# One PSUM bank per sum, out of eight in turn, for the six sums of an FFN input-projection group

## The chip, the cores and the metric

The kernel runs on one core of one Trainium2 chip. The metric is the device time of one execution in microseconds (us), the median of several runs. The names of the engines follow the profile: PE is the matmul engine (PEld its weight load), DVE the vector engine, ACT the scalar engine, POOL and SP the two that mostly issue DMAs here.

## What is computed

One inference step of a two-layer streaming encoder on 1024 prompt frames and 64 frames of a running stream, float32 in and out. Each layer is a mixer (layer 0: Mamba-2 SSD beside a gated short convolution; layer 1: a gated linear recurrence) and then a gated convolutional FFN. The change lies in the FFN, which both layers have:

```python
D_MODEL = 1024; D_FF = 2816; FFN_CONV = 3; DEPTH = 2
def conv_ffn(h, st, w_in, conv_w, conv_b, w_out):
    gu = h @ w_in                                  # (1088, 1024) @ (1024, 5632)
    g, u = gu[..., :D_FF], gu[..., D_FF:]
    g, new_st = causal_dwconv(g, conv_w, conv_b, st)
    return (jax.nn.gelu(g) * u) @ w_out, new_st
x = x + conv_ffn(rmsnorm(x, norm_ffn[l]), ...)
```

## The kernel before, in words

Activations lie transposed, 128 channels on the partitions and T = 1092 tokens along the free dimension (1024 prompt, 4 of padding, 64 of the running stream). Every float32 operand is split into a high and a low half, and each product is three matmuls (high by high, low by high, high by low).

Inside an FFN, `ffn` (L907) goes through 44 half-layers, called **groups** here, 22 in each layer: for each of 11 pairs of 128-channel tiles first a *gate* group (u = 0) and then an *up* group (u = 1). One group multiplies a 2 x 2 block of weight tiles with the two halves of the token axis by a Strassen-Winograd scheme of seven products. The function `seven` (L432) holds it. The products W, Z1, Z2, X1, X2, X3 and Y are each 12 matmuls of 428 columns; V1 and V0 are the 236 tokens left over, each 24 matmuls of 236 columns. That is 84 matmuls of 428 columns and 48 of 236 in a group.

They go to six sums: `pw` (W), `v1` (V1), `v0` (V0), `px` (X1, then X2 on top, then X3 on top), `py` (Y) and `pz` (Z1, then Z2 on top). Before the change the six lie in two PSUM tiles of three banks each, L436 to L438:

```python
        ta, tb = psum(), psum()
        pw, v1, v0 = ta[:, 0, 0:SB], ta[:, 1, 0:RB], ta[:, 2, 0:RB]
        px, py, pz = tb[:, 0, 0:SB], tb[:, 1, 0:SB], tb[:, 2, 0:SB]
```

`psum()` takes from the pool `pm`, which has two such tiles (six of the eight banks); the other two banks are the pool `pa` for `aux()`.

The order of the work is written out by hand. Inside the loop over groups `in_order(True)` (L82) chains the instructions of PE, DVE and ACT to the order of the code, each engine for itself. In a middle group (mode "mid", L484) PE's order is W, V1, Z1, X1, V0, Y, X2, Z2, X3. Between them stand, for DVE and ACT:

- `held(ps)` (L448), an ACT copy of a sum to SBUF (tile `cp`): of `pw` after V1, of `pz` after X1, of `px` after V0 (named p1) and of `px` again after X2 (named u2).
- `plain(m, v)`, a DVE multiplication of `v1` or `v0` into a work tile `wk`.
- `put(m, b, ps, t)`, a DVE addition of a sum and a held copy into `wk`: of `py` and p1 before X2, of `pz` and u2 after Z2, and twice of `px` after X3.
- `nxt.step()` (L397), the next quarter of the next group's weights in tiles `ring`: an ACT copy, a DVE subtraction, and in the first two quarters two more DVE additions. The ring has eight tiles, all eight in use by one group, so that a quarter can be made only when the products that used its tile are through.
- `pending`: what the previous group left, for a gate group its scaling and convolution (`convs`, L931) and its GELU (`gelus`, L942), for an up group the multiplication with the gate and the store to `h_d` (`gated`, L958).

The first group of a layer (mode "first", L504) has another order and holds `rs()`, the RMS norm's sums of squares (matmuls `pa<-ss,ones`) with a chain of ACT and DVE steps behind them (`rstd`, L256). The last group (L528) has another order too. Behind the groups stands the output projection, `chunks` (L570), whose matmuls read `wh` and `wl` and write tiles of `psum()`.

Of the kernel before, what the change touches and what calls it, by code (L numbers as in the profile page):

```python
# [1 line left out]

# [6 lines left out]
F = mybir.dt.float32  # L9
# [4 lines left out]
P = 128  # L14
# [7 lines left out]
NB = 3  # L22
BL = T // NB

SB = 428
RB = T - 2 * SB
# [30 lines left out]
def program(nc, tc, a, ctx):  # L57
# [24 lines left out]
    def in_order(on):  # L82
        order["on"] = on
        for e in (V, S, TE):
            e.last = None
# [2 lines left out]
    sl = ctx.enter_context(tc.tile_pool(name="sl", bufs=1))  # L88
    wp = ctx.enter_context(tc.tile_pool(name="wp", bufs=1))
    sm = ctx.enter_context(tc.tile_pool(name="sm", bufs=1))  # L90
    pm = ctx.enter_context(tc.tile_pool(name="pm", bufs=2, space=bass.MemoryType.PSUM))
    pa = ctx.enter_context(tc.tile_pool(name="pa", bufs=2, space=bass.MemoryType.PSUM))
    dram = ctx.enter_context(tc.tile_pool(name="dram", bufs=1, space=bass.MemoryType.DRAM))

    n_of = {}
# [30 lines left out]

    def psum():
        n_of["pm"] = n_of.get("pm", 0) + 1
        return pm.tile([P, NB, 512], F, tag="pm", name=f"pm{n_of['pm']}")

    def aux():
        n_of["pa"] = n_of.get("pa", 0) + 1
        return pa.tile([P, 4, P], F, tag="pa", name=f"pa{n_of['pa']}")

    def scratch(name, shape):
        return dram.tile(shape, F, name=name, tag=name)
# [47 lines left out]
    def step():  # L184
        if between:
            try:
                next(between[0])
            except StopIteration:
                between.pop(0)
# [115 lines left out]
    class Next:  # L305
# [25 lines left out]
        def rs(self):  # L331
            return rms(self.ss[0], D, self.ss[1])
# [99 lines left out]
    def seven(ws, X, group, pending, nxt, mode="mid", rs=None):  # L432


        put, plain = group
        ta, tb = psum(), psum()  # L436
        pw, v1, v0 = ta[:, 0, 0:SB], ta[:, 1, 0:RB], ta[:, 2, 0:RB]
        px, py, pz = tb[:, 0, 0:SB], tb[:, 1, 0:SB], tb[:, 2, 0:SB]  # L438

        def mul(ps, w, half, name, start=True, ks=range(HK)):  # L440
            for k in ks:
                at = slice((half * HK + k) * P, (half * HK + k + 1) * P)
                wh, wl = ws.w[w][0][:, at], ws.w[w][1][:, at]
                xh, xl = X.part(name, k)
                for i, (wx, x) in enumerate(((wh, xh), (wl, xh), (wh, xl))):
                    TE.matmul(ps, wx, x, start=start and k == 0 and i == 0, stop=k == HK - 1 and i == 2, skip_group_check=True)

        def held(ps):  # L448
            n = n_of["cp"] = n_of.get("cp", 0) + 1
            t = wp.tile([P, 512], F, tag="wh", bufs=4, name=f"cp{n}")[:, 0:SB]  # L450
            S.activation(t, ps, AF.Copy)
            return t

        def V1():
            mul(v1, "a2", 0, "k0")
            mul(v1, "a2", 1, "k1", False)

        def V0():
            mul(v0, "a1", 0, "k0")
            mul(v0, "a1", 1, "k1", False)  # L460

        def W():
            mul(pw, "a2", 1, "t4")

        def Z1():
            mul(pz, "s31", 1, "t1")

        def Z2():
            mul(pz, "s24", 1, "b22", False)

        def X1():
            mul(px, "a1", 0, "b11")

        def X2():
            mul(px, "s24", 0, "t2", False)

        def X3():
            mul(px, "s31", 0, "t3", False)

        def Y():  # L480
            mul(py, "a1", 1, "b21")

        step = nxt.step if nxt is not None else lambda: None
        if mode == "mid":  # L484
            W()
            pending[0]()
            V1()
            w = held(pw)
            Z1()
            pending[1]()  # L490
            plain(1, v1)
            X1()
            p5 = held(pz)
            V0()
            p1 = held(px)
            step()
            plain(0, v0)
            Y()
            step()
            put(0, 0, py, p1)  # L500
            X2()
            u2 = held(px)
            Z2()
        elif mode == "first":  # L504
            ws.step()
            Y()
            mul(v1, "a2", 1, "k1")
            mul(v0, "a1", 1, "k1")
            ws.step()
            for k in range(HK):  # L510
                mul(px, "a1", 0, "b11", True, [k])
                mul(pz, "s31", 1, "t1", True, [k])
                mul(pw, "a2", 1, "t4", True, [k])
                mul(v1, "a2", 0, "k0", False, [k])
                mul(v0, "a1", 0, "k0", False, [k])
            p1 = held(px)
            p5 = held(pz)
            w = held(pw)
            plain(1, v1)
            plain(0, v0)  # L520
            X2()
            put(0, 0, py, p1)
            u2 = held(px)
            rs()
            step()
            step()
            Z2()
        else:  # L528
            Z1()
            pending[0]()  # L530
            X1()
            p5 = held(pz)
            W()
            p1 = held(px)
            pending[1]()
            X2()
            w = held(pw)
            V1()
            u2 = held(px)
            V0()  # L540
            plain(1, v1)
            Y()
            plain(0, v0)
            put(0, 0, py, p1)
            Z2()
        put(0, 1, pz, u2)
        step()
        X3()
        put(1, 0, px, w)
        put(1, 1, px, p5)  # L550
        step()
# [333 lines left out]
    def residual(src):  # L885
        out = []
        for m in Pairs.order:
            t = ring()
            nc.gpsimd.dma_start(t, src(m))
            out.append((m, t))  # L890
        return [t for _, t in sorted(out, key=lambda x: x[0])]
# [15 lines left out]
    def ffn(layer, X, done, after):  # L907

        kind = f"ffn{layer}"
# [7 lines left out]
        def gate(p, first):  # L917
            cbs = [conv_buffer(), conv_buffer()]
            gs = [None, None]

            def put(m, b, ps, t):
                V.tensor_add(cbs[m][:, PAD + b * SB:PAD + (b + 1) * SB], ps, t)

            def plain(m, ps):
                cb = cbs[m][:, PAD + 2 * SB:PAD + T]
                if first:
                    S.activation(cb, ps, AF.Copy)
                else:
                    V.tensor_mul(cb, ps, state["rs"][:, B[2]])

            def convs():  # L931
                RS = state["rs"]
                at = slice(0, T if first else 2 * SB)
                for cb in cbs:
                    V.tensor_mul(cb[:, PAD:][:, at], cb[:, PAD:][:, at], RS[:, at])
                for m, cb in enumerate(cbs):
                    gs[m] = wk()
                    conv_first(cb, kind, 2 * p + m, gs[m])
                for m, cb in enumerate(cbs):
                    conv_rest(cb, kind, 2 * p + m, gs[m])  # L940

            def gelus():  # L942
                for g in gs:
                    S.activation(g, g, AF.Gelu_apprx_tanh)
                    V.tensor_mul(g, g, state["rs"])

            return (put, plain), (convs, gelus), gs
# [22 lines left out]
        def ready(g):  # L970
            p, u = g
            return Ready(*[("f_in", layer, 2 * (2 * p + m) + u) for m in range(2)])

        ws = X.first
        gs, pending = None, (nothing, nothing)
        in_order(True)
        for n, (p, u) in enumerate(groups):
            nw = ready(groups[n + 1]) if n + 1 < len(groups) else None
            if u == 0:
                group, then, gs = gate(p, n == 0)  # L980
            else:
                group, then = up(p, gs)
            seven(ws, X, group, pending, nw, "first" if n == 0 else "last" if nw is None else "mid", rs)
            ws, pending = nw, then
        pending[0]()
        in_order(False)

        XR = residual(lambda m: X.spill[m])
        done.XR = XR
# [16 lines left out]
    x_d = scratch("x_d", [KT, P, T])  # L1006
    last, nxt = nxt, Next(None, "mix1", x_d)
    ffn(0, last, nxt, lambda: prefetch(("lru_in", 8)))


# [157 lines left out]
    for k in keep:  # L1168
        nc.gpsimd.dma_start(a["o_keep_" + k], keep[k].rearrange("p a b c -> p (a b c)"))
    nc.gpsimd.dma_start(a["o_lru"], keep_lru.rearrange("p a b -> p (a b)"))  # L1170

# [102 lines left out]


def build(nc, arrays):
    from contextlib import ExitStack

    ap = {k: nc.dram_tensor(k, v.shape, F, kind="ExternalInput").ap() for k, v in arrays.items()}
    for k, s in OUTS.items():
        ap[k] = nc.dram_tensor(k, s, F, kind="ExternalOutput").ap()
    with tile.TileContext(nc) as tc, ExitStack() as ctx:
        program(nc, tc, ap, ctx)
# [8 lines left out]
```

## Time and profile before

| | us |
|---|---|
| median of 3 runs (3172.82 to 3180.51) | 3174.36 |
| the profiled execution | 3177.55 |
| its span, from the first to the last instruction | 3175.7 |
| PE busy, of the span | 2811.9 (89%) |
| DVE busy | 1894.3 (60%) |
| ACT busy | 971.3 (31%) |

The profiled execution is 3.2 us (0.1%) above the median. The profile gives for each engine the time in which it ran instructions; a busy PE can still run at the lower of its two clocks, and the row PEclk shows the granted clock in tenths of the full one in 40 slices of the span. The two stretches of the FFN input projections lie at 815 to 1538 us and 2163 to 2892 us of the span.

### The profile page before, as it was taken

The page shows a single profiled execution, that of the slowest core. Times are in us where ns is not written, and L with a number is a line of the kernel's source. Part 1 is how long each engine was busy: PE and PEld are TensorE (multiplying, and loading weights), DVE is VectorE, ACT ScalarE, POOL GpSimd, SP SyncE. Part 2 cuts the span into 40 slices and gives each one's busy share as a digit, 9 for nine tenths or more (in the row PEclk, how much of TensorE's full clock was granted, in tenths as well). Part 3 has the DMA queues.
Part 4 walks back from the last instruction along what each step waited for, and adds up shares of the span by engine and source line. Part 5 has one row for each costly group of instructions (what it writes and reads, how often), then busy time and mean ns, then how long its engine had stood idle before and what let it go on. Part 6 is the DMA issues. An engine that isn't in the chain of part 4 may idle for free.

```text
span 3175.7 us, 38882 instructions
## 1 busy us (share of the span) xinstructions
PE 2811.9 (89%) x16132; PEld 2687.4 (85%) x16132; DVE 1894.3 (60%) x2199; ACT 971.3 (31%) x1296; POOL 248.5 (8%) x641
## 2 busy tenths in 40 slices
PE   8999999999877777787999999997777777879998
PEld 8999999999767776676999899997676776769997
DVE  8556566686744455454666676866444454446666
ACT  6333232222422222222211444624222222222212
POOL 1101001110100000000100100201000000001002
PEclk9999999999989898898999999998898898989999
DMA  3222222441311111111532411343111111115222
GB/s 118 85 89 80 76 78 80 143 160 64 109 48 62 48 54 41 41 68 42 192 99 68 139 55 55 103 148 103 48 68 42 49 47 41 69 41 188 95 70 70
DMA packets 81089, 260.16 MB, mean 82 GB/s; under 512 B 9584, under 2 KB 12192, under 8 KB 80912
## 3 DMA queue, kind: packets, MB, share of 16 engines
q0 software_dynamic: 35264, 133.86, 12.6%
q1 hardware_dynamic: 45360, 123.39, 11.9%
q8 instruction: 127, 2.08, 0.3%
q10 hardware_dynamic: 288, 0.42, 0.0%
q14 instruction: 50, 0.41, 0.0%
HBM read 190.36 MB, written 57.21 MB: 78 GB/s over the span
## 4 chain that ended last, share of the span: by engine, by line
PE 72%; DVE 15%; ACT 5%; issue 5%; DMA 2%; POOL 1%; DVEq 0%; SPq 0%; ACTq 0%; POOLq 0%
PE pm L70 70%; DVE wk L70 8%; DVE ring L70 3%; PE pa L70 2%; DVE raw L70 2%; ACT ring L70 2%; DVE x L70 1%; ACT wk L70 1%; ACT x L70 1%; ACT cp L70 1%; DMA wk<-h_d 1%; ACT L70 0%; DVE ss L70 0%; DMA ss<-wk 0%; DMA ring<-at_d 0%
## 5 line engine op out<-in xcount | busy, mean ns | idle before, releaser
L70 PE MATMUL pm<-x,ring 128*128 128x428 f32 (+1 forms) x5808 | 1116.4, 356 | 321.5 <-DVE wk L70 285.2
L70 PEld LDWEIGHTS pm<-x,ring 128*128 128x128 f32 x5808 | 1022.9, 210 | 413.7 <-DVE wk L70 242.9
L70 PE MATMUL pm<-x,wh 128*128 128x364 f32 x6144 | 1228.3, 331 | 7.3 <-DVE ring L70 5.4
L70 PEld LDWEIGHTS pm<-x,wh 128*128 128x128 f32 x6144 | 1043.9, 188 | 17.9 <-DVE ring L70 7.1
L70 PE MATMUL pm<-x,wl 128*128 128x364 f32 x3072 | 684.6, 329 | 0.6 <-DVE wl L70 0.6
L70 PEld LDWEIGHTS pm<-x,wl 128*128 128x128 f32 x3072 | 536.1, 188 | 1.3 <-DVE wl L70 0.9
L70 DVE TENSOR_TENSOR ring<-ring,pm 128x1092 f32<-128x1092 f32 (+2 forms) x273 | 332.3, 1222 | 197.0 <-PE pm L70 192.7
L70 DVE TENSOR_TENSOR wk<-pm,cp 128x428 f32<-128x428 f32 x176 | 101.8, 599 | 404.9 <-PE pm L70 404.9
L70 DVE TENSOR_TENSOR ring<-raw,ring 128x1024 fp32r<-128x1024 f32 x176 | 215.1, 1222 | 198.6 <-ACT ring L70 198.3
L70 ACT ACTIVATE ring<-raw 128x1024 fp32r<-128x1024 f32 x176 | 186.0, 1058 | 425.4 <-PE pm L70 407.5
L70 ACT ACTIVATE cp<-pm 128x428 f32<-128x428 f32 x176 | 87.1, 521 | 501.2 <-PE pm L70 497.2
L70 ACT ACTIVATE wh<-rawo 128x512 fp32r<-128x512 f32 x136 | 84.6, 626 | 352.2 <-PE pm L70 315.0
L70 ACT ACTIVATE wh<-raw 128x512 fp32r<-128x512 f32 x128 | 79.1, 626 | 336.2 <-PE pm L70 335.9
L70 ACT ACTIVATE x<-wk 128x1092 fp32r<-128x1092 f32 (+1 forms) x82 | 87.9, 1072 | 238.7 <-PE pm L70 202.8
L70 DVE SCALAR_TENSOR_TENSOR wk<-wk,par,wk 128x1092 f32<-128x1092 f32 x104 | 138.9, 1353 | 13.8 <-ACT wk L70 12.3
L70 DVE TENSOR_TENSOR wk<-wk,ss 128x1092 f32<-128x1092 f32 (+1 forms) x105 | 123.3, 1196 | 0.2
L70 DVE TENSOR_TENSOR x<-wk,x 128x1092 fp32r<-128x1092 f32 (+1 forms) x82 | 101.9, 1243 | 31.2 <-ACT x L70 31.2
L70 DVE TENSOR_TENSOR wk<-pm,ss 128x236 f32<-128x236 f32 (+1 forms) x75 | 61.1, 815 | 84.7 <-PE pm L70 40.8
L70 DVE TENSOR_TENSOR wl<-raw,wh 128x512 fp32r<-128x512 f32 x128 | 86.5, 682 | 40.4 <-ACT wh L70 40.4
L70 DVE TENSOR_TENSOR wl<-rawo,wh 128x512 fp32r<-128x512 f32 x136 | 91.0, 686 | 28.6 <-ACT wh L70 28.6
L70 ACT ACTIVATE wk<-wk 128x1092 f32<-128x1092 f32 x59 | 65.9, 1117 | 82.3 <-DVE wk L70 78.9
L70 DVE TENSOR_TENSOR wk<-pm,wk 128x236 f32<-128x236 f32 (+1 forms) x60 | 38.3, 641 | 86.5 <-PE pm L70 84.6
(185 smaller groups left out, 1672.3 us busy)
## 6 DMA issues: line engine op xcount, KB each, us to landing
raw<-f_in SPq DMA_DIRECT2D x88, 512.0 KB, 3.5
h_d<-wk POOLq DMA_DIRECT2D x44, 546.0 KB, 4.3
wk<-h_d POOLq DMA_DIRECT2D x42, 546.0 KB, 5.0
raw<-ab_in SPq DMA_DIRECT2D x44, 512.0 KB, 3.6
rawo<-f_out SPq DMA_DIRECT2D x88, 256.0 KB, 3.1
ss<-wk POOLq DMA_DIRECT2D x18, 546.0 KB, 5.1
ring<-at_d POOLq DMA_DIRECT2D x16, 546.0 KB, 7.0
rawo<-ab_out SPq DMA_DIRECT2D x32, 256.0 KB, 3.1
```

The source lines that it names most:

```text
L70: out = call(*args, **kwargs)
```

## The change

The six sums of a group become six tiles of one bank each, taken in turn from a pool `pb` of eight. The pools of PSUM are now opened and closed on the way: `psum_of("seven")` closes `pm` and `pa` and opens `pb` ahead of the groups of a layer, `psum_of("plain")` goes back behind them. `aux()` takes a bank of `pb` meanwhile, so that `rs()` in the first group uses three of the eight.

```diff
-    pm = ctx.enter_context(tc.tile_pool(name="pm", bufs=2, space=bass.MemoryType.PSUM))
-    pa = ctx.enter_context(tc.tile_pool(name="pa", bufs=2, space=bass.MemoryType.PSUM))
+    banks = {"stack": None, "n": 0}
+
+    def psum_of(kind):
+
+        if banks["stack"] is not None:
+            banks["stack"].close()
+        banks["stack"], banks["kind"] = ExitStack(), kind
+        banks["n"] += 1
+        for name in ("pm", "pa") if kind == "plain" else ("pb",):
+            banks[name] = banks["stack"].enter_context(tc.tile_pool(name=f"{name}_{banks['n']}", bufs=2, space=bass.MemoryType.PSUM, reuse_waits="tile"))
+
+    psum_of("plain")
...
+    def bank():
+        n_of["pb"] = n_of.get("pb", 0) + 1
+        return banks["pb"].tile([P, 512], F, tag="pb", bufs=8, name=f"pb{n_of['pb']}")
 
     def aux():
+        if banks["kind"] != "plain":
+            return bank().rearrange("p (a b) -> p a b", a=4)
...
         put, plain = group
-        ta, tb = psum(), psum()
-        pw, v1, v0 = ta[:, 0, 0:SB], ta[:, 1, 0:RB], ta[:, 2, 0:RB]
-        px, py, pz = tb[:, 0, 0:SB], tb[:, 1, 0:SB], tb[:, 2, 0:SB]
+        pw, v1, pz, px, v0, py = [bank()[:, 0:n] for n in (SB, RB, SB, SB, RB, SB)]
...
         in_order(True)
+        psum_of("seven")
         for n, (p, u) in enumerate(groups):
...
         in_order(False)
+        psum_of("plain")
```

No instruction is added or removed, and inside the groups the order on each engine is the same. What differs is the waits, and the place of nine matmuls at the end of a layer. The rows below are PE's order of instructions as built: operation, output, operands, size, and the engines whose semaphores it waits for (DVE_49, Activation_49). A sum's tile is `pm_` before and `pb_` now, `x_` is an activation tile, `ring_` a weight tile.

PE, second group of layer 0 (an up group), from the end of X1 to the start of V0, before:

```order
L70 MATMUL pm_7369<-x_7125,ring_7322 128x428
L70 MATMUL pm_7369<-x_7126,ring_7321 128x428
L70 MATMUL pm_7368<-x_6772,ring_7321 128x236 [waits DVE_49,Activation_49]
L70 MATMUL pm_7368<-x_6772,ring_7322 128x236
L70 MATMUL pm_7368<-x_6773,ring_7321 128x236
```

and now:

```order
L72 MATMUL pb_7380<-x_7125,ring_7331 128x428
L72 MATMUL pb_7380<-x_7126,ring_7330 128x428
L72 MATMUL pb_7381<-x_6772,ring_7330 128x236
L72 MATMUL pb_7381<-x_6772,ring_7331 128x236
L72 MATMUL pb_7381<-x_6773,ring_7330 128x236
```

V0's first matmul waited for DVE and ACT, readers of other banks of its tile; it has no wait now.

PE, the same group, from the end of Z2 to the start of X3, before:

```order
L70 MATMUL pm_7369<-x_7121,ring_7341 128x428
L70 MATMUL pm_7369<-x_7122,ring_7340 128x428
L70 MATMUL pm_7369<-x_6772,ring_7342 128x428 [waits DVE_49]
L70 MATMUL pm_7369<-x_6772,ring_7343 128x428
L70 MATMUL pm_7369<-x_6773,ring_7342 128x428
```

and now:

```order
L72 MATMUL pb_7379<-x_7121,ring_7350 128x428
L72 MATMUL pb_7379<-x_7122,ring_7349 128x428
L72 MATMUL pb_7380<-x_6772,ring_7351 128x428 [waits Activation_49]
L72 MATMUL pb_7380<-x_6772,ring_7352 128x428
L72 MATMUL pb_7380<-x_6773,ring_7351 128x428
```

X3 waited for a DVE reader (the `put` of `pz`); it waits for ACT alone now (the copy u2 of `px`). At X2 the same change is made: the wait for DVE (the `put` of `py`) gives way to one for ACT (the copy p1). At Z2 and Y a wait for ACT is gone.

PE, end of layer 0, from the last matmuls of Z2 on, before:

```order
L70 MATMUL pm_11105<-x_7121,ring_11081 128x428
L70 MATMUL pm_11105<-x_7122,ring_11080 128x428
L70 MATMUL pm_11323<-x_11296,wh_11315 128x364 [waits Activation_49]
L70 MATMUL pm_11323<-x_11296,wh_11315 128x364 x2
L70 MATMUL pm_11323<-x_11296,wl_11316 128x364 [waits DVE_49]
L70 MATMUL pm_11323<-x_11296,wl_11316 128x364 x2
L70 MATMUL pm_11323<-x_11297,wh_11315 128x364 [waits DVE_49]
L70 MATMUL pm_11323<-x_11297,wh_11315 128x364 x2
L70 MATMUL pm_11105<-x_6772,ring_11082 128x428 [waits DVE_49]
```

and now, from the last matmuls of X3 on:

```order
L72 MATMUL pb_11196<-x_7123,ring_11172 128x428
L72 MATMUL pb_11196<-x_7124,ring_11171 128x428
L72 MATMUL pm_11423<-x_11396,wh_11415 128x364 [waits DVE_49,Activation_49]
L72 MATMUL pm_11423<-x_11396,wh_11415 128x364 x2
L72 MATMUL pm_11423<-x_11396,wl_11416 128x364 x3
```

Nine matmuls of the output projection stood ahead of the last X3; they stand behind it now, and the first of them waits for readers of the banks. On POOL the two last stores of `h_d` come a few DMAs earlier than before among the loads of the output projection; SP's order is the same.

## Rows read from the trace of the kernel before

**Rows 1.** The page: the granted clock in 40 slices, in tenths.

```profile
PEclk9999999999989898898999999998898898989999
```

**Rows 2.** Windows of both layers: first two groups, next 18, the end.

```profile
core 0: us, PE busy (x) PEld busy (x) DVE busy (x) ACT busy (x) POOL busy (x), PEclk, DMA share, GB/s
815.14:893.14 78.00, 57.48 (x265) 51.17 (x264) 42.09 (x51) 26.27 (x35) 3.46 (x11) 0.82 0.19 49
2163.49:2241.28 77.79, 55.64 (x266) 49.89 (x265) 41.99 (x51) 27.36 (x36) 3.49 (x11) 0.85 0.17 48
893.14:1476.41 583.27, 451.35 (x2376) 414.03 (x2376) 294.83 (x342) 150.63 (x181) 21.17 (x91) 0.91 0.15 51
2241.28:2831.88 590.60, 458.73 (x2376) 420.69 (x2376) 294.87 (x342) 150.60 (x181) 19.55 (x91) 0.89 0.15 51
1476.41:1537.75 61.34, 51.96 (x286) 47.35 (x287) 31.26 (x36) 17.20 (x22) 6.77 (x18) 0.94 0.34 121
2831.88:2891.91 60.03, 51.77 (x286) 47.37 (x287) 31.28 (x36) 17.22 (x22) 6.76 (x18) 0.94 0.33 117
```

**Rows 3.** PE, layer 0, same stretches: count | busy, mean ns | idle, releasers.

```profile
L70 PE MATMUL pm<-x,ring 128*128 128x428 f32 (+1 forms) x252 | 54.0, 383 | 19.7 <-DVE wk L70 15.1 <-ACT x L70 3.2 <-DVE x L70 0.7
...
L70 PE MATMUL pm<-x,ring 128*128 128x428 f32 (+1 forms) x2376 | 451.4, 353 | 131.9 <-DVE wk L70 120.8 <-ACT cp L70 11.1
...
L70 PE MATMUL pm<-x,ring 128*128 128x428 f32 (+1 forms) x276 | 50.1, 340 | 9.0 <-DVE wk L70 6.5 <-ACT ring L70 1.0 <-DVE ring L70 0.9
```

**Rows 4.** PE's timeline, two groups: start, length, instructions [idle before, releaser].

```profile
1022.48 17.33 PE L70 MATMUL pm<-x,ring 128*128 128x428 f32 x108 [0.77 <-DVE wk L70]
1043.98 4.65 PE L70 MATMUL pm<-x,ring 128*128 128x428 f32 x12 [4.17 <-DVE wk L70]
1049.24 2.61 PE L70 MATMUL pm<-x,ring 128*128 128x428 f32 x12 [0.62 <-ACT cp L70]
1052.62 12.31 PE L70 MATMUL pm<-x,ring 128*128 128x428 f32 x72 [0.77 <-DVE wk L70]
1068.44 6.89 PE L70 MATMUL pm<-x,ring 128*128 128x236 f32 x36 [3.51 <-DVE wk L70]
1079.51 4.15 PE L70 MATMUL pm<-x,ring 128*128 128x428 f32 x12 [4.17 <-DVE wk L70]
1084.27 2.59 PE L70 MATMUL pm<-x,ring 128*128 128x428 f32 x12 [0.62 <-ACT cp L70]
```

**Rows 5.** Windows: the output projection of layer 0, and an X2.

```profile
1534.60:1786.00 251.40, 251.37 (x1503) 250.91 (x1504) 161.96 (x153) 49.63 (x66) 13.75 (x26) 1.00 0.31 107
1043.98:1048.63 4.65, 4.65 (x12) 3.82 (x12) 0.00 (x0) 0.00 (x0) 0.00 (x0) 0.50 0.00 0
```

**Rows 6.** One pair of groups: its window, two groups each of DVE and ACT.

```profile
1087.63:1152.71 65.08, 50.47 (x264) 46.38 (x265) 32.76 (x38) 16.72 (x21) 2.13 (x10) 0.90 0.15 50
...
L70 DVE TENSOR_TENSOR ring<-raw,ring 128x1024 fp32r<-128x1024 f32 x8 | 9.8, 1222 | 9.8 <-ACT ring L70 9.8
...
L70 DVE TENSOR_TENSOR wk<-pm,cp 128x428 f32<-128x428 f32 x8 | 4.6, 598 | 18.0 <-PE pm L70 18.0
...
L70 ACT ACTIVATE ring<-raw 128x1024 fp32r<-128x1024 f32 x9 | 9.5, 1058 | 21.9 <-PE pm L70 21.9
L70 ACT ACTIVATE cp<-pm 128x428 f32<-128x428 f32 x8 | 4.0, 520 | 23.7 <-PE pm L70 23.7
```

**Rows 7.** PE's timeline in the first group of layer 0.

```profile
839.53 4.15 PE L70 MATMUL pa<-ss,ones 128*128 128x364 f32 x12
...
852.42 3.93 PE L70 MATMUL pm<-x,ring 128*128 128x428 f32 x10 [6.40 <-DVE wk L70]
```

**Rows 8.** DVE's timeline at the end of layer 0: the last two puts.

```profile
1537.79 1.11 DVE L70 TENSOR_TENSOR wk<-pm,cp 128x428 f32<-128x428 f32 x2 [0.89 <-PE pm L70]
```

**Rows 9.** DMA issues: KB of one, median us from issue to landing.

```profile
raw<-f_in SPq DMA_DIRECT2D x88, 512.0 KB, 3.5
h_d<-wk POOLq DMA_DIRECT2D x44, 546.0 KB, 4.3
```

More of the change, by code (lines that the diff above doesn't have):

```diff
@@ L1 @@
+from contextlib import ExitStack
 import numpy as np
@@ L128, in psum @@
         n_of["pm"] = n_of.get("pm", 0) + 1
-        return pm.tile([P, NB, 512], F, tag="pm", name=f"pm{n_of['pm']}")
+        return banks["pm"].tile([P, NB, 512], F, tag="pm", name=f"pm{n_of['pm']}")
+    def bank():
+        n_of["pb"] = n_of.get("pb", 0) + 1
+        return banks["pb"].tile([P, 512], F, tag="pb", bufs=8, name=f"pb{n_of['pb']}")
     def aux():
+        if banks["kind"] != "plain":
+            return bank().rearrange("p (a b) -> p a b", a=4)
         n_of["pa"] = n_of.get("pa", 0) + 1
-        return pa.tile([P, 4, P], F, tag="pa", name=f"pa{n_of['pa']}")
+        return banks["pa"].tile([P, 4, P], F, tag="pa", name=f"pa{n_of['pa']}")
     def scratch(name, shape):
@@ L1170, in program @@
     nc.gpsimd.dma_start(a["o_lru"], keep_lru.rearrange("p a b -> p (a b)"))
+    banks["stack"].close()
 def tiles_of(w):
@@ L1278, in build @@
 def build(nc, arrays):
-    from contextlib import ExitStack
     ap = {k: nc.dram_tensor(k, v.shape, F, kind="ExternalInput").ap() for k, v in arrays.items()}
```

## The prediction

> **What bounds the kernel now.** The page comes first: in its 40 slices PE's granted clock reads 9, which is full or nearly, except in two stretches where slices of 8 and 9 alternate [rows 1]. Those are the input projections of the two FFNs, so I read them alone, in windows: two first groups, 18 groups in the middle, and the last two with the change to the output projection [rows 2]. Together they last 1451.0 us, DVE is busy for half of that, ACT for 27%, and the granted clock is 0.82 to 0.94 of the full one. PE's own groups say what it waits for: in the 18 middle groups of layer 0 it sat idle for 131.9 us, 120.8 of them until a DVE instruction and 11.1 until an ACT copy was done, and for no weight or activation [rows 3].
>
> The timeline shows where [rows 4]. A gate group and an up group last 65.1 us (from the X3 at 1022.48 to the X3 that ends the pair). PE runs X3 to Y of the gate group without a pause (108 matmuls), waits 4.17 us ahead of X2, 0.62 ahead of Z2 and 0.77 ahead of X3; in the up group it waits 3.51 ahead of V0, and then the same three again. Sum 14.63 us a pair; nine pairs give 131.7, all of the 131.9. So each of the seven rows is one wait of the pattern.
>
> Are they needed? X2 adds onto `px`, so it has to wait for the copy p1 of `px`. But the wait ended at DVE, with the `put` of `py`, another bank of the same tile. X3 needs the copy u2 of `px` and waited for the `put` of `pz`; V0 needs nothing and waited for the reader of `v1`; Z2 needs nothing late and waited for u2. The waits go by tile, not by bank. PE's rows of order, in the part on the change, agree: with a tile to each sum V0 has no wait left, and X2 and X3 wait for ACT alone.
>
> The waits cost more than their length. X2 takes 4.65 us behind its 4.17 us wait at a granted clock of 0.50 [rows 5], which is 1.2 of 2.4 GHz, and the same twelve matmuls take 2.6 us in Z2 [rows 4]. In long stretches without waits the chip grants 1.00: 1503 matmuls of the output projection in 251.4 us [rows 5].
>
> **The change, part by part.** Time of a group at the full clock, from the uninterrupted runs [rows 4]: 108 matmuls (60 of 428 columns, 48 of 236) take 17.33, 72 (48 and 24) 12.31, 12 of 428 take 2.60, each with a tail t for the last one's end. Twice the difference of the first two is 24a + 48b = 10.04; then 36a + t = 7.29 and 12a + t = 2.60 give a = 0.195 us for 428 columns, t = 0.26, b = 0.112 for 236. A group is 84a + 48b = 21.77 us, a pair 43.5 instead of 65; twelve matmuls of 428 columns are 2.34.
>
> The Trainium skill ("TensorE: Matmul & The Clock Gate", Back-to-back issue gap) gives N/2.4 + 2.5 ns between warm matmuls, 0.181 and 0.101 us here, for a stream without weight loads of its own. By that, an estimate from the page, a group would be 20.0 us and my sum some 76 us lower; every matmul here has its own weight load, and 108 in a row show 0.195 and 0.112, so I stay with the rows and give the other no chance.
>
> *Middle groups.* 36 groups, now 583.27 + 590.60 = 1173.9 us [rows 2]; 36 x 21.77 = 783.7. **Gain 390.2**, if nothing else becomes late. What could: (a) X2 behind p1: the copy (0.52 us, from X1's end) has V0 and Y as cover, 5.0 us. (b) X3 behind u2: Z2 covers with 2.34. (c) Z1 of the next group reads the last quarter of the weights, an ACT copy that must wait for X3's end (1.06) and a DVE subtraction of 1.22 behind the two puts of 0.6 [rows 6]; with some 0.3 for the tail and the hand-overs about 2.8 us, covered by W and V1 with 5.0. (d) DVE: 32.8 us busy in a pair [rows 6] of 43.5, and ACT 16.7. (e) The weights' loads, 3.5 us each [rows 9], start when that last quarter is done, some 3 us behind X3's end, and are wanted at the copy after X1, 9.7 behind it. (f) The stores of `h_d`, 4.3 us [rows 9], hold back a work tile and so a `plain` on DVE, not PE. (g) Eight banks, six a group: a bank comes back after eight sums, so Y takes the bank of the previous group's `px`, read by the two puts right behind X3, 12 us and more earlier. The smallest cover, (b), has less than 2 us to spare; where one is gone, each microsecond a group costs 36.
>
> *First two groups*, 78.0 and 77.8 us [rows 2]. Without waits they would be 2 x 21.77 less an X3, 41.2. What stays: the waits for the activations, 3.2 + 0.7 [rows 3]; the norm's matmuls, which stand in this stretch, 4.1 [rows 7]. Of the 15.1 us of waits for DVE [rows 3] a part only changes place: the 6.40 ahead of X3 [rows 7] comes from a DVE queue filled by the norm's chain and two quarters of weights, and this work remains. X3 no longer waits for it, but the weights behind it (Z1 of the next group) and, by way of convolution and GELU, p1 do. Between 0 and 15 I take 9, the row's 6.40 and 2.6 for the chain through p1, and 3 for matmuls at the lower clock behind such waits. 41.2 + 3.9 + 4.1 + 9 + 3 = 61.2; **gain 155.8 - 122.4 = 33**.
>
> *End*, 61.3 and 60.0 us [rows 2]: floor 2 x 21.77 + 2.34 = 45.9. The waits for the last group's weights, 1.0 + 0.9 [rows 3], stay. Nine matmuls of the output projection move behind the last X3: they were inside this stretch, 9 x 0.167 (251.4 / 1503 [rows 5]) = 1.5 us, and are now outside. They also covered the handover: the new tile of three banks has to wait for the last two puts, 1.11 us that start 0.3 behind X3 [rows 8]; with the tails I set 2.3 between X3 and the first of them, nothing as the lower bound. 45.9 + 1.9 + 1.5 + 2.3 = 51.6; **gain 121.4 - 103.2 = 18**. Opening `pb` ahead of the first group makes the first product wait for the old sums to be read; the 3.2 us wait for the activations right behind it takes that in. SP's order is unchanged, and POOL's earlier stores are not waited for.
>
> Sum: 390 + 33 + 18 = 441 us. The profiled execution took 3177.55 (its span 3175.7), so I expect **2736 us**; the median of the runs shown is 3.2 lower, which I leave in the range. By itself this forecast reaches from 2707 (nothing of the DVE queue, the lower clock and the handover stays: 2 x (9 + 3 + 2.3) less) to 2773 (each of the 36 middle groups keeps one wait like that ahead of X3, 0.77 and a restart of 0.26).
>
> **The rivals.** *The waits go, the clock does not come back.* PE could still pause for tenths of a microsecond at each change of bank, and the chip could grant what it does now. Then a pair is 65.1 - 14.6 = 50.5 us, 7.0 above my 43.5, and 18 pairs put the time at 2736 + 126 = 2862. For it: the clock fell two or three times in each pair. Against it: in rows 4 each slow product follows a wait of over 3 us, and Z2 behind 0.62 runs at full speed. The Trainium skill has this as a rule (the same page, "A second HAM failure mode: psum-queue depth-cycling"): a kernel that cycled through PSUM banks had its clock swing by such micro-idles; here the runs behind the short waits speak against it. Chance 5%.
>
> *DVE or ACT becomes the bound.* DVE is busy 32.8 us in a pair and waits 9.8 for ACT's copies of the weights [rows 6]: 42.6, just under PE's 43.5. If half of the 18.0 us for which it now waits for sums stayed too, a pair would be 51.6 and the time 2736 + 18 x 8.1 = 2882. Against it: those waits shorten with PE, as the sums come sooner. Chance 6%.
>
> *Nothing happens*: another tile or wait holds PE at the same places, 3177. The order speaks against it. 2%.
>
> *Slower: the lower clock for good.* Denser work could make the chip hold 1.2 GHz through these stretches. X2's 4.65 against 2.61 is a factor of 1.78; a group would take 38.8 us, 44 of them 1705 against 1451 now, and the time 3177 + 254 = 3431. It decides once a group is above 1451 / 44 = 33.0 us, that is, with about two thirds of the columns at the lower clock. Against it: 1.00 over 251 us [rows 5]. 2%.
>
> **How the numbers follow.** Forecast 85%, then 5, 6, 2 and 2%. The forecast's own range, with 3 us on top for the median and the unequal runs, already holds over 8 in 10: 2707 to 2776. About 0.3%, 10 us, is what a measurement of this kernel can tell from no change. Faster: 85 + 5 + 6 = 96%; same 2%; slower 2%.
>
> **What would show it.** Right: in the 18 middle groups PE's idle time from DVE falls from 120.8 us to nearly nothing, the granted clock reads 1.00, and a pair takes 43.5 us with DVE at three quarters busy. The start of a layer keeps waits for DVE, of which the longest is ahead of Z1 in the second group, and lasts about 61 us; the first matmul of the output projection waits about 2 us behind X3. Wrong: short idle rows with a clock of 0.9 (first rival), DVE near 100% in these windows with PE waiting for `ring` (second), or runs of matmuls slower than 0.195 and 0.112 us at full clock, which would break the floor itself.

## The result and the profile after

| | before | change |
|---|---|---|
| median, us | 3177.44 (4 runs, 3172.82 to 3184.90) | 2731.84 (4 runs, 2729.15 to 2733.08) |
| profiled execution, us | 3177.55 | 2729.15 |
| its span, us | 3175.7 | 2727.4 |

The ratio of the times is 0.8595, with a 95% interval of 0.8575 to 0.8614. The forecast was 2736 us, 6.9 above the profiled execution and 4.2 above the median.

The page of the changed kernel: busy time by engine, and the granted clock in the 40 slices, which read 9 throughout now (before, 8 and 9 alternated in two stretches [rows 1]).

```profile
PE 2663.2 (98%) x16132; PEld 2602.0 (95%) x16132; DVE 1890.9 (69%) x2199; ACT 972.7 (36%) x1296; POOL 248.8 (9%) x641
...
PEclk9999999999999999999999999999999999999999
```

The six stages in windows, cut at the same instructions and with the same columns as [rows 2]; the last row is the 22 us behind the last X3 of layer 0, of which more below.

```profile
818.87:870.21 51.34, 47.01 (x264) 43.61 (x265) 35.10 (x43) 24.09 (x32) 3.46 (x11) 0.97 0.19 58
1940.54:1998.00 57.46, 50.09 (x265) 45.54 (x265) 39.18 (x47) 26.44 (x35) 3.49 (x11) 0.91 0.25 66
870.21:1260.93 390.72, 390.72 (x2377) 380.73 (x2376) 295.28 (x346) 151.87 (x180) 19.48 (x91) 1.00 0.22 76
1998.00:2388.78 390.78, 390.78 (x2377) 380.62 (x2376) 295.29 (x346) 151.85 (x180) 20.23 (x91) 1.00 0.23 76
1260.93:1309.22 48.29, 46.42 (x277) 44.30 (x275) 29.33 (x35) 17.04 (x21) 6.24 (x17) 1.00 0.36 124
2388.78:2438.73 49.95, 48.07 (x277) 45.68 (x275) 30.52 (x36) 18.13 (x22) 6.24 (x17) 0.97 0.36 121
1309.22:1331.50 22.28, 18.99 (x106) 19.02 (x106) 16.72 (x18) 5.54 (x8) 5.79 (x11) 0.92 0.96 359
```

PE's matmuls of the products in layer 0, first groups, middle and end (count | busy us, mean ns | idle us before, releasers); [rows 3] are the same of before.

```profile
L72 PE MATMUL pb<-x,ring 128*128 128x428 f32 (+1 forms) x252 | 43.9, 334 | 8.2 <-DVE ring L72 5.9 <-ACT cp L72 1.4 <-ACT ring L72 0.9
...
L72 PE MATMUL pb<-x,ring 128*128 128x428 f32 (+1 forms) x2377 | 391.1, 327 | 0.0
...
L72 PE MATMUL pb<-x,ring 128*128 128x428 f32 (+1 forms) x277 | 46.6, 329 | 1.9 <-ACT ring L72 1.0 <-DVE ring L72 0.9
```

In the middle PE waited for nothing in 390.72 us, where it had waited 131.9; busy time and window are the same number, and the clock reads 1.00. A group takes 390.72 / 18 = 21.71 us, against 583.27 / 18 = 32.40. DVE does the same work as before, 295 us, and is busy for 76% of the window.

The span went from 3175.7 to 2727.4, 448.3 us, by stages:

| stage | before | after | difference |
|---|---|---|---|
| from the span's start to the first product of layer 0 | 815.1 | 818.9 | +3.7 |
| first two groups, both layers | 155.8 | 108.8 | -47.0 |
| 18 middle groups, both layers | 1173.9 | 781.5 | -392.4 |
| end of the groups, both layers | 121.4 | 98.2 | -23.1 |
| from the last X3 of layer 0 to the first product of layer 1 | 625.7 | 631.3 | +5.6 |
| behind the last X3 of layer 1 | 283.8 | 288.7 | +4.9 |

Two stages became longer. At the entry of layer 0, the changed kernel's first product waits for the last reader of an old sum. The timeline of PE in the first two groups of layer 0 (start, length, instruction, count [idle before, releaser]) begins with that wait:

```profile
818.87 18.61 PE L72 MATMUL pb<-x,ring 128*128 128x428 f32 x108 [3.89 <-DVE ring L72]
837.32 3.83 PE L72 MATMUL pb<-ss,ones 128*128 128x364 f32 x12
840.71 10.12 PE L72 MATMUL pb<-x,ring 128*128 128x428 f32 x60
851.73 0.46 PE L72 MATMUL pb<-x,ring 128*128 128x428 f32 x1 [0.90 <-ACT ring L72]
854.20 9.79 PE L72 MATMUL pb<-x,ring 128*128 128x428 f32 x59 [2.01 <-DVE ring L72]
865.42 6.90 PE L72 MATMUL pb<-x,ring 128*128 128x428 f32 x34 [1.42 <-ACT cp L72]
```

The reader is an addition on DVE that takes an old sum (`pm`) and ends at 818.72, 0.15 us ahead of the product:

```profile
817.44 1.28 DVE L72 TENSOR_TENSOR ring<-ring,pm 128x1092 f32<-128x1092 f32 x1
```

The waits for activations that stood in this stretch, 3.2 and 0.7 us [rows 3], are gone from it, so that the 3.9 us have only changed place. In layer 1 the first product starts without a wait, and the two waits for activations stay (3.36 and 0.73 us). At the other end, behind X3, the output projection's first matmul waits 3.29 us in layer 0 (first row, PE) for the last two puts of DVE (the last row of the fence after it), which wait behind two instructions of DVE that make the output projection's activations (`x`, the rows above):

```profile
1312.51 0.74 PE L72 MATMUL pm<-x,wh 128*128 128x364 f32 x3 [3.29 <-ACT wh L72]
```

```profile
1308.84 1.30 DVE L72 TENSOR_TENSOR x<-wk,x 128x1092 fp32r<-128x1092 f32 x1 [1.31 <-ACT x L72]
1310.06 1.29 DVE L72 TENSOR_TENSOR x<-ss,x 128x1092 fp32r<-128x1092 f32 x1
1311.26 1.11 DVE L72 TENSOR_TENSOR wk<-pb,cp 128x428 f32<-128x428 f32 x2
```

The profile names an ACT copy of `wh` as the releaser; the puts end at 1312.37, 0.14 ahead of the matmul. That it was the puts is settled by the last experiment.

### The profile page after: what moved, and what is told of

It is laid out like the page before. It is cut to its first block, busy times and chain, and to the rows that moved or that the text cites. A ratio compares the mean times of both kernels' runs of the same rounds, so it can differ in the third digit from the quotient of the medians.

```text
span 2727.4 us, 38829 instructions
## 1 busy us (share of the span) xinstructions
PE 2663.2 (98%) x16132; PEld 2602.0 (95%) x16132; DVE 1890.9 (69%) x2199; ACT 972.7 (36%) x1296; POOL 248.8 (9%) x641
## 3 DMA queue, kind: packets, MB, share of 16 engines
q0 software_dynamic: 35264, 133.86, 14.6%
## 4 chain that ended last, share of the span: by engine, by line
PE 85%; DVE 5%; issue 4%; ACT 3%; DMA 3%; POOL 1%; SPq 0%; DVEq 0%; POOLq 0%; ACTq 0%
PE pm L72 50%; PE pb L72 33%; PE pa L72 3%; DVE x L72 1%; ACT x L72 1%; DVE ring L72 1%; DVE wk L72 1%; DMA ss<-wk 1%; ACT wk L72 1%; DMA wk<-h_d 1%; DVE ss L72 1%; ACT L72 0%; DMA x<-x 0%; DMA wk<-ysc_d 0%; ACT ring L72 0%
## 5 line engine op out<-in xcount | busy, mean ns | idle before, releaser
L72 PE MATMUL pb<-x,ring 128*128 128x428 f32 (+1 forms) x5808 | 966.6, 328 | 19.3 <-DVE ring L72 10.0
L72 PEld LDWEIGHTS pb<-x,ring 128*128 128x128 f32 x5808 | 936.1, 190 | 49.2 <-DVE ring L72 7.5
L72 ACT ACTIVATE cp<-pb 128x428 f32<-128x428 f32 x176 | 89.9, 522 | 241.8 <-PE pb L72 239.4
L72 DVE TENSOR_TENSOR wk<-pb,cp 128x428 f32<-128x428 f32 x176 | 101.6, 599 | 50.0 <-PE pb L72 31.6
L72 ACT ACTIVATE wk<-wk,par 128x1092 f32<-128x1092 f32 x52 | 65.3, 1296 | 66.2 <-DVE wk L72 48.6
L72 DVE TENSOR_TENSOR wk<-pm,ss 128x1092 f32<-128x1092 f32 x35 | 45.1, 1290 | 55.2 <-PE pm L72 40.5
```

What stands on the lines that cost most here:

```text
L72: out = call(*args, **kwargs)
```

## The experiments

The theory: the time lay in seven waits a pair that existed because a sum shared its tile with others, in the restart behind each (some 0.26 us, the tail t of the prediction), and in the matmuls that ran at the lower clock behind the long ones; with a tile to each sum PE is the bound, with some room under DVE and ACT. The rivals: the gain comes from the new handling of the pools (opened and closed on the way, with `reuse_waits`) or from eight banks instead of six; short pauses pull the clock down as long ones do; DVE is as good as the bound already. All times for a stage are the 18 middle groups of layer 0 (583.27 before, 390.72 in the change).

### The pools switched as in the change, the tiles as before

```diff
-        for name in ("pm", "pa") if kind == "plain" else ("pb",):
+        for name in ("pm", "pa"):
...
-        pw, v1, pz, px, v0, py = [bank()[:, 0:n] for n in (SB, RB, SB, SB, RB, SB)]
+        ta, tb = psum(), psum()
+        pw, v1, v0 = ta[:, 0, 0:SB], ta[:, 1, 0:RB], ta[:, 2, 0:RB]
+        px, py, pz = tb[:, 0, 0:SB], tb[:, 1, 0:SB], tb[:, 2, 0:SB]
```

> The pools are opened and closed as in the change, but a group's six sums lie in two tiles of three banks as before. Theory (all of the gain is the tile to each sum): the time of before, 3165 to 3195 us, with 14.6 us of waits a pair again. Rival (the way the pools are opened gives part of the gain): below 3140.

Measured: 3178.54 us in one run, 3185.14 before on the same chip. The middle groups take 583.89 us, and PE's row is that of before again:

```profile
L72 PE MATMUL pm<-x,ring 128*128 128x428 f32 (+1 forms) x2377 | 452.4, 353 | 132.7 <-DVE wk L72 121.6 <-ACT cp L72 11.1
```

So the gain is the tiles', not that of opening and closing pools, which this kernel does in the same way.

### Two sums in one tile, three ways

Three kernels put one pair of sums back into a shared tile of two banks (two such tiles) and leave the other four sums a bank each, out of four. This is the edit for `pz` and `px`; the others share `px` with `py`, and `v1` with `v0`. Each was run once.

```diff
-        return banks["pb"].tile([P, 512], F, tag="pb", bufs=8, name=f"pb{n_of['pb']}")
+        return banks["pb"].tile([P, 512], F, tag="pb", bufs=4, name=f"pb{n_of['pb']}")
...
-        pw, v1, pz, px, v0, py = [bank()[:, 0:n] for n in (SB, RB, SB, SB, RB, SB)]
+        tw = banks["pb"].tile([P, 2, 512], F, tag="pw2", bufs=2, name=f"pw{n_of.get('pb', 0)}")
+        pz, px = tw[:, 0, 0:SB], tw[:, 1, 0:SB]
+        pw, v1, v0, py = [bank()[:, 0:n] for n in (SB, RB, RB, SB)]
```

> Only pz and px share a tile, the other four sums have a bank each. Theory (a short wait costs its length and a restart, the clock stays): Z2 waits 0.62 and X3 0.77 again, each with a restart of 0.26, 1.9 us a group: the 18 middle groups of layer 0 go from 390.7 to 425 us at a granted clock of 1.00, the whole to 2816. Rival (short pauses at a change of bank make the clock swing): a clock near 0.90 in these groups, 465 us or more for them and 2900 or more in all.

Measured: 2820.58 us. The window of the 18 groups, PE's row of the shared tile, and the timeline of Y, Z2 and the X3 that follows:

```profile
882.59:1307.96 425.37, 400.49 (x2377) 377.80 (x2377) 293.46 (x342) 150.87 (x181) 21.04 (x91) 1.00 0.21 70
```

```profile
L72 PE MATMUL pw<-x,ring 128*128 128x428 f32 x1081 | 226.4, 360 | 25.6 <-DVE wk L72 14.6 <-ACT cp L72 11.1
```

```profile
1017.89 2.51 PE L72 MATMUL pw<-x,ring 128*128 128x428 f32 x12
1021.02 2.61 PE L72 MATMUL pw<-x,ring 128*128 128x428 f32 x12 [0.62 <-ACT cp L72]
1024.39 2.60 PE L72 MATMUL pw<-x,ring 128*128 128x428 f32 x12 [0.77 <-DVE wk L72]
```

The two short waits are back, at their old lengths, in each group. They cost 425.37 - 390.72 = 34.65 us, 1.92 a group: 25.6 / 18 = 1.42 of waits and 0.50 for two restarts, close to twice the tail of 0.26. The clock stays at 1.00 and the matmuls behind the waits run at full speed. For pauses of this length the rival in which they pull the clock down falls; the last section shows slightly longer ones behind which it fell.

The Trainium skill ("TensorE: Matmul & The Clock Gate", A second HAM failure mode: psum-queue depth-cycling) speaks of a clock that swings with micro-idles while a kernel cycles through PSUM banks. The middle groups do not show that: this kernel with 36 short pauses in 18 groups kept 1.00, and so did the change with its turn of eight banks and no pause.

> Only px and py share a tile. Theory (a long wait costs its length and then matmuls at the lower clock): X2 waits 4.17 again, with a restart of 0.26 and some 1.8 us of matmuls at 1.2 GHz, 6.2 us a group: 500 to 525 us for the 18 middle groups, 2995 to 3030 in all, granted clock about 0.9. Rival (the lower clock costs nothing of its own): 4.4 us a group, 470 and 2927.

Measured: 2990.73 us, just under the expected range; the middle groups 505.69, inside it.

```profile
881.28:1386.97 505.69, 428.02 (x2377) 408.15 (x2376) 293.33 (x342) 151.88 (x180) 20.38 (x91) 0.93 0.18 59
...
1014.88:1018.72 3.84, 3.84 (x13) 3.59 (x14) 0.00 (x0) 0.00 (x0) 0.00 (x0) 0.63 0.00 0
```

```profile
L72 PE MATMUL pw<-x,ring 128*128 128x428 f32 x864 | 209.9, 399 | 77.7 <-DVE wk L72 77.7
```

```profile
1008.20 2.50 PE L72 MATMUL pw<-x,ring 128*128 128x428 f32 x12
1014.88 3.84 PE L72 MATMUL pw<-x,ring 128*128 128x428 f32 x12 [4.18 <-DVE wk L72]
```

X2's wait for the put of `py` alone costs (505.69 - 390.72) / 18 = 6.39 us a group, of which 77.7 / 18 = 4.32 are the wait. The other 2.07 are the restart and the lower clock: X2 takes 3.84 us at a granted clock of 0.63, the same twelve matmuls of X1 2.50.

> Only v1 and v0 share a tile. Theory: V0 waits for the reader of v1, which is late only in up groups, behind the previous group's convolution and GELU on DVE: 3.5 us, a restart and 1.8 us at the lower clock, 5.6 us in 22 of 44 groups: 441 us for the 18 middle groups and 2855 in all; gate groups stay at 21.7 us. Rival (the shared tile holds up both kinds of group): 490 us and 2975.

Measured: 2852.42 us, the middle groups 443.23 at a clock of 0.95.

```profile
881.86:1325.09 443.23, 412.53 (x2377) 399.37 (x2377) 295.01 (x342) 151.89 (x180) 20.74 (x91) 0.95 0.20 67
```

```profile
L72 PE MATMUL pw<-x,ring 128*128 128x236 f32 x864 | 121.4, 304 | 30.7 <-DVE wk L72 30.7
```

```profile
1006.81 2.85 PE L72 MATMUL pw<-x,ring 128*128 128x236 f32 x24
...
1017.75 5.47 PE L72 MATMUL pw<-x,ring 128*128 128x236 f32 x24 [3.41 <-DVE wk L72]
```

Only the up groups wait, as before: 30.7 / 9 = 3.41 us each, and V0 behind it takes 5.47 us where V1 takes 2.85. Together that is 52.5 us in nine groups (443.23 - 390.72).

The three kernels hold between them all seven waits of a pair, and they nearly add up: 34.7 + 115.0 + 52.5 = 202.2 us, where before was 192.5 above the change. By these shares about 57% of the gain in the middle groups is X2's wait, 26% V0's and 17% those of Z2 and X3. Of the 10 us by which the parts exceed the whole, 1.3 are idle time of PE and 8.3 its busy time; why is open.

### Six banks, one for each sum, not in turn

```diff
-        pw, v1, pz, px, v0, py = [bank()[:, 0:n] for n in (SB, RB, SB, SB, RB, SB)]
+        pw, v1, pz, px, v0, py = [own(t)[:, 0:n] for t, n in (("pw", SB), ("v1", RB), ("pz", SB), ("px", SB), ("v0", RB), ("py", SB))]
```

`own` gives each name a tile of one bank with a single buffer, and `aux()` keeps its two banks.

> Each sum has one fixed bank of its own, six in all, and none are taken in turn; the other two banks stay with the auxiliary tiles. Theory (a tile to each sum is what counts; the px bank comes free 1.4 us behind X3 and is wanted again 7.4 us behind it): as the change, 2724 to 2740 us, 390 to 392 us for the 18 middle groups of layer 0. Rival (the turn of eight is needed): X1 waits for the last two puts of the group before, at least 1 us a group, 409 us and 2775 or more.

Measured: 2729.51 us (2727.99 to 2731.18, 4 runs), ratio to before (3181.03 on the same chip) 0.8581 (0.8562 to 0.8600).

```profile
871.81:1262.53 390.72, 390.72 (x2378) 380.71 (x2377) 295.30 (x346) 151.91 (x180) 19.55 (x91) 1.00 0.23 76
```

The middle groups take what they take in the change, to the hundredth of a microsecond. The turn of eight banks gives nothing here; one tile to a sum is what counts.

### More work for DVE

One kernel repeats, and another makes four times in all, the DVE subtraction behind the last quarter of a group's weights, a step whose repetition gives the same values. This is the first; the second has `range(3)`.

```diff
             ready(*last[1])
+            (h, l), raw = self.w[last[1][0]], last[1][1]
+            for _ in range(1):
+                V.tensor_sub(l, raw, h.bitcast(F))
             yield
```

> The change, with the DVE subtraction of the last quarter of the weights done twice: 1.22 us more on DVE in each group, ahead of Z1 of the next. Theory A (what counts is the chain from X3's end to Z1, 2.8 us now under a cover of 5.0): 4.0 us, still covered, 391 us for the 18 middle groups and 2728 to 2740 in all. Theory B (DVE's queue as a whole is nearly the bound: 32.8 us busy and 9.8 waiting for ACT in a pair of 43.5): 35.2 + 9.8 = 45.0 a pair, 405 us and 2765.

Measured: 2739.23 us (2737.03 to 2741.76, 4 runs), ratio 0.8612 (0.8592 to 0.8632), an interval that overlaps the change's. In the middle nothing moved; the same wait of Z1 in the first groups as above is longer by the added instruction, 3.26 for 2.01. Outside the middle the addition does cost something: all four runs lie above those of the six banks, measured beside it (2727.99 to 2731.18), by 9.7 us in the medians.

```profile
875.03:1265.75 390.72, 390.72 (x2377) 380.75 (x2377) 313.72 (x362) 151.94 (x180) 18.96 (x91) 1.00 0.22 76
```

```profile
858.69 21.48 PE L72 MATMUL pb<-x,ring 128*128 128x428 f32 x110 [3.26 <-DVE ring L72]
```

> The same with three more of these subtractions, 3.66 us on DVE in each group. Theory A: the chain takes 6.5 us under a cover of 5.0, so 1.5 us and a restart a group, 422 us for the 18 middle groups and 2808 in all. Theory B: 40.1 + 9.8 = 49.9 us a pair, 449 us and 2873.

Measured: 2836.06 us (2835.59 to 2838.09, 4 runs), ratio 0.8917 (0.8894 to 0.8941).

```profile
877.77:1308.75 430.98, 401.92 (x2377) 383.71 (x2376) 356.13 (x395) 150.03 (x180) 20.57 (x91) 0.99 0.20 69
```

```profile
L72 PE MATMUL pb<-x,ring 128*128 128x428 f32 (+1 forms) x2377 | 402.3, 330 | 29.1 <-DVE ring L72 29.1
```

```profile
1007.58 22.25 PE L72 MATMUL pb<-x,ring 128*128 128x428 f32 x132 [0.91 <-DVE ring L72]
1032.27 17.91 PE L72 MATMUL pb<-x,ring 128*128 128x428 f32 x101 [2.44 <-DVE ring L72]
```

All of PE's idle time is now ahead of Z1, for the low halves of its weights, by turns 0.91 and 2.44 us. So the cover of W and V1 over the last quarter of the weights holds for one more DVE instruction of 1.22 us and not for three. The size was off: 40.26 us of added time are 2.24 a group, where theory A had 1.5 and a restart; 29.1 / 18 = 1.62 of them are the wait, the rest restarts and matmuls at the lower clock (the window's reads 0.99). Theory B's 449 us were not reached, but by its own count DVE is close to full: busy for 356 of 431 us, and waiting for ACT's copies of the weights for most of the rest.

```profile
L72 DVE TENSOR_TENSOR ring<-raw,ring 128x1024 fp32r<-128x1024 f32 x126 | 154.1, 1223 | 59.4 <-ACT ring L72 57.5
```

What theory B had wrong is that this waiting would stay at 9.8 us a pair: here it is 57.5 / 9 = 6.4.

### The output projection's first tile in the other banks

```diff
-        for name in ("pm", "pa") if kind == "plain" else ("pb",):
-            banks[name] = banks["stack"].enter_context(tc.tile_pool(name=f"{name}_{banks['n']}", bufs=2, space=bass.MemoryType.PSUM, reuse_waits="tile"))
+        for name in ("pm0", "pm1", "pa") if kind == "plain" else ("pb",):
+            banks[name] = banks["stack"].enter_context(tc.tile_pool(name=f"{name}_{banks['n']}", bufs=1 if name[:2] == "pm" else 2, space=bass.MemoryType.PSUM, reuse_waits="tile"))
+        banks["turn"] = 0
...
-        return banks["pm"].tile([P, NB, 512], F, tag="pm", name=f"pm{n_of['pm']}")
+        banks["turn"] = 1 - banks["turn"]
+        return banks[f"pm{banks['turn']}"].tile([P, NB, 512], F, tag="pm", name=f"pm{n_of['pm']}")
```

> The change, with the two tiles of three banks of the plain stretches in turn from the other one on, so that the output projection begins in banks 3 to 5, whose sums are read early, and not in the bank of px. Theory (the handover is held by the next weights and activations too): the wait of 3.3 us ahead of the first matmul of the output projection goes and comes back a few matmuls later ahead of the next weights; about as much idle time of PE in the 10 us behind the last X3, 2726 to 2738 in all. Rival (the last puts alone hold the handover): under 1 us of idle time there, and 5 to 7 us less in all.

Measured: 2730.33 us (2726.92 to 2731.18, 4 runs), ratio 0.8581 (0.8562 to 0.8601). PE behind the last X3 of layer 0:

```profile
1313.77 0.77 PE L72 MATMUL pm<-x,wh 128*128 128x364 f32 x3 [0.42 <-ACT x L72]
...
1317.33 0.76 PE L72 MATMUL pm<-x,wh 128*128 128x364 f32 x3 [0.96 <-DVE wk L72]
...
1319.85 0.77 PE L72 MATMUL pm<-x,wl 128*128 128x364 f32 x3 [1.59 <-DVE wl L72]
```

The first matmul waits 0.42 instead of 3.29 us, and now for an activation, so in the change the banks were what it lacked, and not `wh` or an activation. The second tile then waits for the puts and the next for `wl`, whose making stands behind those puts on DVE. Sum 2.97 against 3.29: the wait has moved, and the time with it by less than the runs can tell. No version here is measurably faster than the change.

## Why the prediction was right

**The middle groups** were forecast at 21.77 us each and a gain of 390.2; they took 21.71, and the gain was 392.4. The floor, 0.195 and 0.112 us for a matmul, was right to 0.3%. The Trainium skill's gap ("TensorE: Matmul & The Clock Gate", Back-to-back issue gap), 20.0 us a group as an estimate, is too short for this stream with a weight load to every matmul: the measured 21.71 decides. The covers (a) to (g) held: PE has no idle row. (c) is the one that was tested: it holds for 1.22 us more and breaks with 3.66 more. Of the gain, 131.9 us a layer are waits; the other 392.4 - 2 x 131.9 = 128.6 are restarts and lower clock, and for layer 0 the three kernels with one shared pair show it wait by wait.

**The first two groups** were forecast at 61.2 us each. They took 51.34 and the 3.73 us of later start in layer 0, 55.1 in all, and 57.46 in layer 1. The term that was mis-sized is the 9 us for the DVE queue. I carried over the whole 6.40 us that X3 had waited [rows 7], but the 60 matmuls in front of Z1, X3, W and V1 among them, run meanwhile: Z1 waits 0.90 us for the high and 2.01 for the low halves of its weights, and p1's chain adds 1.42, so 4.3 in layer 0; in layer 1 it is 3.3, without a wait for p1. The places were as forecast. For the lower clock I had 3; PE's busy time, 47.01 and 50.09, is above the 41.2 of the products and 3.4 of the norm's matmuls (837.32 to 840.71) by 2.4 us in layer 0 and 5.5 in layer 1, restarts included.

**The end and the handover** were forecast together, at a gain of 18; the end gave 23.1 and what stands behind it took 10.5 back, so 12.6. Half of the miss is the handover: 1.5 for the nine moved matmuls and 2.3 of wait in each layer, 3.8, became 5.6 and 4.9. In layer 0 the wait is 3.29, since two DVE instructions of 1.3 us for the next activations came in ahead of the puts, which I had put right behind X3; in layer 1 it is 2.1. Left out was a restart at the lower clock, which came in layer 0: the first 6.0 us of the output projection, 27 matmuls, have a granted clock of 0.72 (last section), and at 0.167 each they would take 4.5. In layer 1 the clock there is 1.00, and some 1.3 of the 4.9 us stay unexplained. The other half of the miss lies ahead of X3's end: floor and waits for weights were forecast at 45.9 + 1.9 = 47.8 us in each layer and took 48.29 and 49.95, the latter with a stretch at the lower clock behind two pauses of 0.95 and 0.93 us (last section).

**The sum**: 392.4 + 43.3 (the first groups less the later start) + 12.6 = 448.3 measured, 390 + 33 + 18 = 441 forecast. Two errors of opposite sign, 10 and 5 us, remain beside a main term that was right by 2; that they partly cancel is luck, but the main term would have carried the forecast without it.

**The rivals**: the clock came back in the middle groups, with and without short pauses; DVE has 1.22 us a group to spare at the narrowest place and did not become the bound; the tiles were the cause; and 390 us of unbroken matmuls were granted 1.00, so dense work did not lower the clock.

## What to carry to other kernels

Where PE waits ahead of a product for a reader of a sum that it doesn't touch, look whether the two sums share a tile: the waits go by tile, and one tile to a sum took away 14.6 us of waits in a pair of 65 without another bank being needed. Price such a wait by its row and add the restart, and, where the row behind it is slow, the time lost at the lower clock; here that made 131.9 us of waits worth 192.5 in layer 0. A wait that only changes place is worth its length less what PE does on the way to the new place, and a queue that was carried over whole, at 9 us, cost 4.3 and 3.3.

## What the runs showed of the hardware

The cost of a pause was far from proportional to its length. Behind 0.62 and 0.77 us the granted clock stayed at 1.00 and the only loss was about 0.25 us; a 3.41 us wait made the next 24 matmuls take 5.47 us for 2.85, and one of 4.18 us left X2 at 0.63. Nor does the length alone decide. The rows below are windows of the change that begin where a wait ends. The clock read 1.00 behind Z1's pauses of 0.90 and 2.01 us in layer 0, but 0.57 behind those of 1.03 and 2.01 at the same place of layer 1 (rows 1 and 2). In the last group of a layer Z1's pauses of 0.96 and 0.92 us left 1.00 in layer 0, and those of 0.95 and 0.93 left 0.57 in layer 1 (rows 3 and 4). Behind the 3.29 us at the handover of layer 0 it read 0.72 (row 5):

```profile
854.20:858.20 4.00, 4.00 (x20) 3.87 (x21) 2.59 (x3) 1.56 (x2) 1.72 (x6) 1.00 0.61 210
...
1982.01:1986.01 4.00, 4.00 (x13) 3.76 (x14) 2.58 (x3) 1.56 (x2) 1.74 (x6) 0.57 0.64 185
...
1287.43:1291.43 4.00, 4.00 (x20) 3.86 (x21) 3.50 (x4) 2.90 (x3) 0.00 (x0) 1.00 0.50 164
2415.31:2419.31 4.00, 4.00 (x13) 3.77 (x14) 3.50 (x4) 2.50 (x3) 0.00 (x0) 0.57 0.51 168
...
1312.51:1318.51 6.00, 6.00 (x27) 6.00 (x28) 4.10 (x6) 0.53 (x2) 3.68 (x7) 0.72 0.87 308
```

What tells the pauses that cost the clock from those that do not was not found: a price from one row need not hold at the next. Also unforeseen was how exactly PE set the time once it had no wait: the change, the kernel with six fixed banks and the one with 18 us more of DVE work all took 390.72 us for the 18 middle groups of layer 0.
